# A hybrid decoder layer: attention scores in two fp32r passes, residual spilled, out-projection by tile

## Chip, cores and metric

The kernel runs on one core of a Trainium2 chip. The metric is the device time of one execution in microseconds (us). A TensorE matmul streams up to 512 columns through 128 rows of stored weights; VectorE, ScalarE and GpSimd work on tiles of 128 partitions; DMA queues move tiles between DRAM and SBUF. Every engine carries out its own instructions strictly in the order of its queue and waits for the others through semaphores.

## The reference

One decoder layer of 512 tokens and width 1024 in float32. The mixer in the middle is what the change touches:

```python
x = layer_norm(alpha * x + 0.5 * swiglu_ffn(x, ffn1_w13, ffn1_w2), ln1_g, ln1_b)
gq, gk, gv, gz, ga, gb, dq, dk, dv = jnp.split(x @ w_in, offsets, axis=-1)
y_a = gdn_mixer(gq, gk, gv, gz, ga, gb, ...)         # gated delta rule, 4 heads x 128, gate silu(z)
y_b = diff_attention_mixer(dq, dk, dv, ...)          # 4 heads, two softmax maps of 64 dims each
x = layer_norm(alpha * x + concat(y_a, y_b) @ w_out, ln2_g, ln2_b)
...                                                  # second FFN with a gated embedding, LN3

# diff_attention_mixer, for one block of 128 queries
s = einsum("bqhmd,bkhmd->bhmqk", q, k) * 64 ** -0.5  # m: two maps
s = where(causal, s, -inf); pr = softmax(s, axis=-1)
attn = pr[:, :, 0] - lam * pr[:, :, 1]
o = rms_norm(einsum("bhqk,bkhd->bqhd", attn, v), subln_w) * (1 - lam_init)
```

## The kernel before

The 512 tokens are four tiles of 128 (`NT`). Large products run in three fp32r matmuls (`mm3`, L295 to L299): operands are split into a rounded high part (a ScalarE cast) and the remainder (a VectorE subtract), and hi x hi, hi x lo, lo x hi add up in PSUM. Small products run as fp32 matmuls, each of which the trace shows as two passes.

Three stages follow one another: the first FFN (until about 362 us), the mixers (until about 689 us), the second FFN. At the end of the first, `norm_natural` normalises each token tile in `RES[t]` with VectorE, ScalarE and GpSimd (L302 to L326) and `norm_turn` (L341) transposes it on TensorE.

The mixers (`mix_zone`, L823) begin with the values and gates, then `keys_queries` (L958): for each head a product of 24 matmuls, a convolution on VectorE and a silu on ScalarE into `KQ`, and one unit later `squares`, which turns the unit before (`turn4`, L871) and squares it. What follows is woven from lanes. A lane is a Python generator that yields an estimated cost and a wait; `weave` (L97) takes the first open lane whose time has come, and so fixes the order in which the code is emitted. The framework's scheduler and the rotating buffers (PSUM tags a, b, c of 3, 2 and 3 tiles; 3 raw weight tiles, 4 split ones) then set the order within each engine. The lanes:

- `gdn(c)` (L1057): four chunks of the delta rule; `diagonal` (L1111) inverts 16x16 blocks with 30 VectorE operations (L1129, L1130), going through DRAM before (`ST<-blocks`, L1123) and after (`TT<-blocks`, L1137); `chain` (L1194) carries the state over the chunks (L1202 to L1249) and hands each chunk to `to_mix`, which turns and splits it into `XH`, `XL`.
- `attention(t, h)` (L1144): 16 lanes, one for a query tile and a head. Two scores (L1156, on 64 rows each, keys in `DKT`, queries in `DQT`) and their mask (L1157), the maxima (L1158), exponentials (L1161), difference (L1165), transposes (L1169), the product with `DV` (L1175), a norm with a power on GpSimd (L1182) and the output y (L1183), written over the query.
- `fill` (L995): the projections of keys, queries, values and z, block by block. A key or query tile is rotated on GpSimd, turned on TensorE and copied on VectorE (L1003).
- `out_attn` (L1276) after all heads: four turns, then the attention half of the output product; `out_gdn` (L1285) after it: the other half, LN2.

`TT` (32 rows of blocks, cleared by GpSimd at L851) and `DQT` have tiles of their own. Weights come over SP's DMA queue in order; DMAs of the diagonal go over SP and ScalarE's queue.

## Time and profile before

| | us |
|---|---|
| time, median of three runs (lowest, highest) | 1088.29 (1087.98, 1088.46) |
| the profiled execution | 1089.54 |
| its span on the core | 1087.8 |
| mean granted TensorE clock | 0.998 |

The page gives for each engine the time in which it had an instruction under way. Matmuls overlap in TensorE's pipeline, so a matmul's price is read from the distance between two starts, not from its duration. PE is TensorE, PEld its weight loads, DVE VectorE, ACT ScalarE, POOL GpSimd, SP the queue of most DMAs; an x2 behind an fp32 matmul is its two passes. Idle time stands in brackets or behind "idle", with the instruction that ended it.

### The profile page before, as it was taken

Reading aid. Unit: us, or ns where it says so; the run is one execution under the profiler, and the core shown is the slowest. Engines: PE = TensorE matmul, PEld = TensorE weight load, DVE = VectorE, ACT = ScalarE, POOL = GpSimd, SP = SyncE. Lnnn points to the kernel's source line nnn. Section 1 sums busy time; section 2 is a strip of 40 time slices with the busy share of each in tenths; the row PEclk is TensorE's granted clock in tenths of the full one; section 3 lists DMA queues with packets and bytes.
Section 4 is the critical chain, followed back from the end, with each engine's and each line's share of the span. In section 5 each row is a group of like instructions: output and inputs, shape, how many; then the busy total and the mean of one; then the engine's idle time right before and its main releaser. Section 6 shows DMA issues by size and latency. Waiting matters only on the chain. (4 is left out here: it accounts for less than half of the span.)

```text
span 1087.8 us, 17345 instructions
## 1 busy us (share of the span) xinstructions
PE 1066.9 (98%) x6627; PEld 941.0 (87%) x6627; DVE 827.7 (76%) x1446; ACT 490.8 (45%) x949; POOL 108.6 (10%) x172
## 2 busy tenths in 40 slices
PE   9999999999999999999999999999999999999996
PEld 7889898989897978778865887789899998999895
DVE  5989796979678466357665558899988796979568
ACT  5645353535343266324465632545454453535231
POOL 1100000000002202431112303100000000000003
PEclk9999999999999999999999999999999999999999
DMA  8633232333333042124110211514342433333212
GB/s 290 204 115 118 89 110 94 117 91 109 93 109 106 1 136 87 33 74 108 40 59 1 78 43 54 174 59 146 119 124 79 117 98 90 123 99 98 78 39 97
DMA packets 44275, 106.03 MB, mean 97 GB/s; under 512 B 10848, under 2 KB 12528, under 8 KB 44192
## 3 DMA queue, kind: packets, MB, share of 16 engines
q1 hardware_dynamic: 37968, 96.71, 29.1%
q0 software_dynamic: 1808, 6.04, 1.7%
q10 hardware_dynamic: 4416, 2.16, 0.7%
q8 instruction: 52, 0.85, 0.3%
q14 instruction: 31, 0.25, 0.1%
HBM read 102.41 MB, written 2.49 MB: 96 GB/s over the span
## 5 line engine op out<-in xcount | busy, mean ns | idle before, releaser
L160 DVE TENSOR_TENSOR wl<-raw,wh 128x1024 fp32r<-128x1024 f32 (+3 forms) x137 | 142.8, 1049 | 38.7 <-ACT wh L159 37.5
L159 ACT CAST wh<-raw 128x1024 fp32r<-128x1024 f32 (+3 forms) x137 | 123.0, 905 | 100.3 <-PE pa L298 31.0
L297 PE MATMUL pb<-wh,hh 128*128 128x512 f32 (+1 forms) x356 | 138.5, 390 | 3.7 <-DVE RES L734 1.1
L298 PE MATMUL pb<-wl,hh 128*128 128x512 f32 (+1 forms) x356 | 138.0, 388 | 0.0
L299 PE MATMUL pb<-wh,hl 128*128 128x512 f32 (+1 forms) x356 | 137.8, 387 | 0.0
L229 ACT CAST th<-tr 128x512 fp32r<-128x512 f32 x160 | 98.5, 619 | 85.1 <-PE pc L298 49.8
L233 DVE TENSOR_TENSOR tl<-tr,th 128x512 fp32r<-128x512 f32 x160 | 109.4, 686 | 11.2 <-ACT th L229 10.3
L190 ACT CAST wh<-raw 128x512 fp32r<-128x512 f32 x88 | 54.4, 622 | 134.2 <-PE pb L299 88.1
L297 PE MATMUL pb<-wh,XH 128*128 128x512 f32 (+1 forms) x256 | 101.5, 397 | 1.8 <-ACT wh L159 1.0
L297 PE MATMUL pa<-XH,wh 128*128 128x256 f32 (+1 forms) x344 | 100.0, 291 | 0.1
L298 PE MATMUL pa<-XL,wh 128*128 128x256 f32 (+1 forms) x344 | 100.0, 291 | 0.0
L299 PE MATMUL pa<-XH,wl 128*128 128x256 f32 (+1 forms) x344 | 99.9, 290 | 0.0
L298 PE MATMUL pb<-wl,XH 128*128 128x512 f32 (+1 forms) x256 | 97.6, 381 | 1.2 <-DVE wl L160 1.1
L299 PE MATMUL pb<-wh,XL 128*128 128x512 f32 (+1 forms) x256 | 96.9, 379 | 0.0
L297 PE MATMUL pc<-XH,th 128*128 128x256 f32 x320 | 90.6, 283 | 0.0
L298 PE MATMUL pc<-XL,th 128*128 128x256 f32 x320 | 90.6, 283 | 0.0
L299 PE MATMUL pc<-XH,tl 128*128 128x256 f32 x320 | 90.6, 283 | 0.0
L490 DVE TENSOR_TENSOR RES<-RES,pb 128x512 f32<-128x512 f32 (+1 forms) x81 | 54.6, 677 | 45.2 <-PE pb L299 44.4
L191 DVE TENSOR_TENSOR wl<-raw,wh 128x512 fp32r<-128x512 f32 x88 | 60.2, 690 | 31.7 <-ACT wh L190 31.6
L297 PEld LDWEIGHTS pb<-wh,hh 128*128 128x128 f32 x356 | 66.9, 188 | 19.4 <-DVE RES L734 1.9
L299 PEld LDWEIGHTS pb<-wh,hl 128*128 128x128 f32 x356 | 66.9, 188 | 13.9
L298 PEld LDWEIGHTS pb<-wl,hh 128*128 128x128 f32 x356 | 66.9, 188 | 13.1 <-DVE wl L191 0.3
(312 smaller groups left out, 2665.0 us busy)
## 6 DMA issues: line engine op xcount, KB each, us to landing
raw<-in_wa_dram SPq DMA_DIRECT2D x127, 512.0 KB, 3.7
raw<-in_wb_dram SPq DMA_DIRECT2D x88, 256.0 KB, 2.7
raw<-in_wd_dram SPq DMA_DIRECT2D x4, 520.0 KB, 3.6
RES<-in_xn_dram POOLq DMA_DIRECT2D x4, 512.0 KB, 5.9
gb<-in_gb_dram POOLq DMA_DIRECT2D x8, 256.0 KB, 4.0
xr<-in_xT_dram ACTq DMA_DIRECT2D x7, 256.0 KB, 4.6
out_dram<-RES SPq DMA_DIRECT2D x5, 256.0 KB, 2.1
TT<-in_gb_dram POOLq DMA_DIRECT2D x4, 256.0 KB, 3.6
```

The lines of the kernel that those rows point to most:

```text
L159: return (self.nc.scalar.copy(hi, src), self.nc.vector.tensor_tensor(lo, src, hi.bitcast(F32), ALU.subtract))
L160: self.nc.vector.tensor_tensor(lo, src, hi.bitcast(F32), ALU.subtract))
L190: nc.scalar.copy(hi, r)
L191: nc.vector.tensor_tensor(lo, r, hi.bitcast(F32), ALU.subtract)
L229: act.copy(h, t)
L233: dve.tensor_tensor(hl[1], t, hl[0].bitcast(F32), ALU.subtract)
L297: pe.matmul(o, wh, xh, start=first, stop=False)
L298: pe.matmul(o, wh, xl, start=False, stop=False)
L299: pe.matmul(o, wl, xh, start=False, stop=last)
L490: dve.tensor_tensor(rj, rj, pd, ALU.add)
```

## The change

Scores. `KK` holds for each of the two maps m the high part of the turned keys in this map's 64 rows and the remainder in the other map's rows. `QZ` holds, for four heads in turn, the queries in four slots: slot m has the high part of map m in its own rows and the full query, rounded, in the other rows; slot 2+m has the remainder in its own rows and zeros in the others. A score is then two fp32r matmuls on 128 rows with the same `KK`. `QZ` is written for two heads at once by the even head: two ScalarE casts, two GpSimd casts, two VectorE subtracts. A turned key tile is written by two ScalarE casts and two VectorE subtracts instead of one VectorE copy.

Memory. The residual becomes one tile `RESA`. `TT` lies over its tiles 0 and 1, the queries `DQT` over tiles 2 and 3. So the four residual tiles are stored to DRAM (`XR`) during the third key unit, and loaded again in `out_attn`: 0 and 1 at its start, 2 and 3 after tiles 1 and 3 have been turned. `TT` is cleared after the stores, and the LN2 gains are loaded into `DV` instead of `TT`.

Order. Squares come two units after their unit instead of one; key blocks use PSUM "c"; z is copied and its silu done for two tiles at once; `out_attn` opens when the delta rule's chunks and z are done and takes each tile when its four heads are done; its turns use PSUM "b" and `project_out` yields after every second weight tile; the costs given to `weave` for attention change.

```diff
-        self.RES = [cp.tile([P, D], F32, name=f"RES{t}") for t in range(NT)]
+        self.RESA = cp.tile([P, NT, D], F32, name="RESA")
+        self.RES = [self.RESA[:, t] for t in range(NT)]
...
+        KK = mp.tile([P, 2, H, S], F32R, name="KK")
+        QZ = mp.tile([P, 4, 4, P], F32R, name="QZ")
+        DQT = [self.RESA[:, 2 + t // 2, (t % 2) * 512:(t % 2) * 512 + 512].rearrange("p (h b) -> p h b", b=P)
+               for t in range(NT)]
+        TT = self.RESA[:, 0:2].rearrange("p c (d h b) -> p (c d) h b", d=2, b=P)
...
-        pool.memset(TT, 0.0)
+        XR = dp.tile([NT, P, D], F32, name="XR")
...
-                    if held:
-                        squares(*held)
+                    if len(held) == 2:
+                        squares(*held.pop(0))
...
+                    held.append((i, h))
+                    if i == 0 and h == 2:
+                        for t in range(NT):
+                            nc.sync.dma_start(XR[t], RES[t])
+                    if i == 1 and h == 0:
+                        pool.memset(TT, 0.0)
...
-                    dve.tensor_copy((DKT if word == "k" else DQT)[:, :, t * P:(t + 1) * P], v4(pt))
+                    if word == "k":
+                        for m in range(2):
+                            r, o = rows(m), rows(1 - m)
+                            hi = KK[r, m, :, t * P:(t + 1) * P]
+                            act.copy(hi, v4(pt)[r])
+                            dve.tensor_tensor(KK[o, m, :, t * P:(t + 1) * P], v4(pt)[r], hi.bitcast(F32), ALU.subtract)
+                    else:
+                        dve.tensor_copy(DQT[t], v4(pt))
...
-                    pq = ps("b")
+                    pq = ps("c" if word == "k" else "b")
...
+                act.copy(ZG[:, t], v4(pq))
+                if t % 2:
+                    z = ZG[:, t - 1:t + 1].rearrange("p t h b -> p (t h) b")
+                    act.activation(z, z, AF.Silu)
...
+            i = (t * H + h) % 4
+            qz = QZ[:, i]
+            if h % 2 == 0:
+                two, src = QZ[:, i:i + 2], DQT[t][:, h:h + 2]
+                for m in range(2):
+                    r, o = rows(m), rows(1 - m)
+                    act.copy(two[r, :, m], src[r])
+                    pool.tensor_copy(two[o, :, m], src[r])
+                    dve.tensor_tensor(two[r, :, 2 + m], src[r], two[r, :, m].bitcast(F32), ALU.subtract)
+                said.add(("qz", t, h + 1))
+                yield 0, 2.0
...
-                r = slice(m * DQK, (m + 1) * DQK)
-                pe.matmul(sc[m], DQT[r, h, t * P:(t + 1) * P], DKT[r, h, 0:n], start=True, stop=False)
+                for q in (m, 2 + m):
+                    pe.matmul(sc[m], qz[:, q], KK[:, m, h, 0:n], start=q == m, stop=False)
...
         def out_attn():
-            for t in range(NT):
-                to_mix(DQT[:, :, t * P:(t + 1) * P], t, 4, "c")
-                yield 0.5, 0
+            for t in (0, 1):
+                nc.sync.dma_start(RES[t], XR[t])
             w = [self.take() for _ in range(4)]
             for t in range(NT):
+                while not done[t] <= said:
+                    yield 0, 0.5
+                to_mix(DQT[t], t, 4, "b")
+                if t % 2:
+                    nc.sync.dma_start(RES[2 + t // 2], XR[2 + t // 2])
+                yield 0.5, 1.0
                 yield from project_out(w, 0, t)
...
-        need_out = {("attn",) + th for th in heads} | {"z"}
+        need_out = {("gdn", c) for c in range(NC)} | {"z"}
```

Three places in the order of the instructions. The first is VectorE at the start of attention: the copy of query tile 0 (`DQT`, in `RESA` after), the maxima (`amx`) and the diagonal operations on `ST`. Before:

```order
L1003 COPY DKT<-pb_5080 128x4x128
L1003 COPY DQT<-pb_5119 128x4x128
L1158 TENSOR_REDUCE amx_5132<-pc_5131 128x1
L1129 TENSOR_TENSOR ST_4062<-ST_4061 128x15
L1158 TENSOR_REDUCE amx_5149<-pc_5148 128x1
L1130 TENSOR_TENSOR ST_4061<-ST_4061,ST_4062 128x15
L1129 TENSOR_TENSOR ST_4062<-ST_4061 128x28
L1158 TENSOR_REDUCE amx_5132<-pc_5131 128x1
L1130 TENSOR_TENSOR ST_4061<-ST_4061,ST_4062 128x14x2
```

In the changed kernel, at the place where the copy stands now:

```order
L1153 TENSOR_TENSOR ST_4058<-ST_4057 128x64
L1154 TENSOR_TENSOR ST_4057<-ST_4057,ST_4058 128x8x8
L1153 TENSOR_TENSOR ST_4058<-ST_4057 128x63
L1154 TENSOR_TENSOR ST_4057<-ST_4057,ST_4058 128x7x9
L1022 COPY RESA<-pb_5134 128x512
L1153 TENSOR_TENSOR ST_4058<-ST_4057 128x60
L1154 TENSOR_TENSOR ST_4057<-ST_4057,ST_4058 128x6x10
L1153 TENSOR_TENSOR ST_4058<-ST_4057 128x55
L1180 TENSOR_TENSOR QZ<-RESA,QZ 64x2x128
L1154 TENSOR_TENSOR ST_4057<-ST_4057,ST_4058 128x5x11
L1180 TENSOR_TENSOR QZ<-RESA,QZ 64x2x128
```

The copy L1003, now L1022, stood ahead of the first diagonal operation and now stands behind the eighteenth of them (L1153, L1154); the subtracts into `QZ` (L1180) follow it.

The second is GpSimd at the end of the first FFN, the norms of tiles 2 and 3 (`bnrs`, `RES`) and the clearing of `TT`. Before:

```order
L326 TENSOR_TENSOR RES_70<-RES_70,gb_3795 128x256
L314 TENSOR_TENSOR bnrs_3979<-bnrs_3979,mhalf 128x1
L316 TENSOR_SCALAR bnrs_3979<-bnmv_3977,bnrs_3979 128x1
L325 TENSOR_TENSOR RES_71<-RES_71,gb_3794 128x256
L326 TENSOR_TENSOR RES_71<-RES_71,gb_3795 128x256
L314 TENSOR_TENSOR bnrs_4037<-bnrs_4037,mhalf 128x1
L851 MEMSET TT 128x2048
```

In the changed kernel (`RESA` in L986 is `TT`):

```order
L327 TENSOR_TENSOR RESA<-RESA,gb_3792 128x256
L986 MEMSET RESA 128x2048
L315 TENSOR_TENSOR bnrs_3976<-bnrs_3976,mhalf 128x1
L317 TENSOR_SCALAR bnrs_3976<-bnmv_3974,bnrs_3976 128x1
L326 TENSOR_TENSOR RESA<-RESA,gb_3791 128x256
L327 TENSOR_TENSOR RESA<-RESA,gb_3792 128x256
L315 TENSOR_TENSOR bnrs_4034<-bnrs_4034,mhalf 128x1
```

The memset has moved from behind the last norm to between those of tiles 1 and 2.

The third is TensorE in attention of tile 3. Before, its scores (L1156) stand between the matmuls of the z projection (`pb`):

```order
L297 MATMUL pb_6069<-wh_5427,XH 128x512
L298 MATMUL pb_6069<-wl_5428,XH 128x512
L299 MATMUL pb_6069<-wh_5427,XL 128x512
L297 MATMUL pb_6069<-wh_5729,XH 128x512
L298 MATMUL pb_6069<-wl_5730,XH 128x512
L299 MATMUL pb_6069<-wh_5729,XL 128x512
L1156 MATMUL pc_6048<-DKT,DQT 128x512
L1157 LDWEIGHTS idb
L1157 MATMUL pc_6048<-LVM,idb 128x128
L297 MATMUL pb_6069<-wh_5729,XH 128x512
L1156 MATMUL pc_6049<-DKT,DQT 128x512
L1157 LDWEIGHTS idb
```

In the changed kernel, the scores of the same tile (L1193):

```order
L1239 MATMUL pa_6277<-ST_4058,KQ 128x128 x4
L1247 MATMUL pa_6287<-ST_4058,KQ 128x128 x4
L298 MATMUL pb_6330<-wh_5872,XH 128x512
L299 MATMUL pb_6330<-wl_5873,XH 128x512
L300 MATMUL pb_6330<-wh_5872,XL 128x512
L298 MATMUL pb_6330<-wh_6134,XH 128x512
L299 MATMUL pb_6330<-wl_6135,XH 128x512
L1254 MATMUL pa_6316<-VV,UU 128x128
L300 MATMUL pb_6330<-wh_6134,XL 128x512
L1193 MATMUL pc_6296<-KK,QZ 128x512 x2
L1194 LDWEIGHTS idb
L1194 MATMUL pc_6296<-LVM,idb 128x128
```

Between the scores now stand steps of the chain (L1239, L1247, L1254) and a few matmuls of the output product.

## Rows read from the trace of the kernel before

**Rows 1.** Page, part 1: engine, busy us, share of the span, instructions.
```profile
PE 1066.9 (98%) x6627; PEld 941.0 (87%) x6627; DVE 827.7 (76%) x1446; ACT 490.8 (45%) x949; POOL 108.6 (10%) x172
```

**Rows 2.** Timeline, TensorE: start, duration, line, operation, form, count; scores of tiles 0, 3.
```profile
476.63 0.40 PE L297 MATMUL pb<-wh,XH 128*128 128x512 f32 x1
476.87 0.39 PE L298 MATMUL pb<-wl,XH 128*128 128x512 f32 x1
477.09 0.40 PE L299 MATMUL pb<-wh,XL 128*128 128x512 f32 x1
477.42 0.48 PE L1156 MATMUL pc<-DKT,DQT 64*128 64x128 f32 x2
477.83 0.23 PE L1157 MATMUL pc<-LVM,idb 128*128 128x128 bf16 x1
...
574.75 1.12 PE L1156 MATMUL pc<-DKT,DQT 64*128 64x512 f32 x2
575.81 0.23 PE L1157 MATMUL pc<-LVM,idb 128*128 128x128 bf16 x1
```

**Rows 3.** Timeline, TensorE: the values stage, and eight fp32 passes in gdn.
```profile
359.30 0.28 PE L297 MATMUL pb<-wh,XH 128*128 128x256 f32 x1
359.41 0.28 PE L298 MATMUL pb<-wl,XH 128*128 128x256 f32 x1
...
538.71 1.05 PE L1105 MATMUL pa<-UU,ta 128*128 128x128 f32 x8
539.60 0.60 PE L871 MATMUL pb<-CST,tb 128*128 128x128 f32 x4
```

**Rows 4.** Waits of lines L1156 and L871: TensorE idle until, us, times.
```profile
  DVE DQT L1183: 3.3, 5
...
  ACT KQ L899: 3.9, 7
```

**Rows 5.** Timeline, TensorE, SP, VectorE: diagonal (third row: KB, us to landing).
```profile
468.24 1.46 PE L1071 MATMUL pa<-KQ 128*128 128x256 f32 x6
...
474.10 0.34 SPq L1123 DMA_DIRECT2D ST<-blocks  x1
...
ST<-blocks SPq DMA_DIRECT2D x1, 128.0 KB, 2.8
...
483.65 0.21 DVE L1129 TENSOR_TENSOR ST<-ST 128x63 f32<-128x63 f32 x1
...
484.16 0.22 DVE L1129 TENSOR_TENSOR ST<-ST 128x60 f32<-128x60 f32 x1
```

**Rows 6.** Timeline, GpSimd, TensorE: norms of FFN1 [idle before, releaser].
```profile
355.09 0.98 POOL L314 TENSOR_TENSOR bnrs<-bnrs,mhalf 128x1 f32<-128x1 f32 x1 [1.81 <-DVE bnrs L313]
...
358.53 0.73 POOL L326 TENSOR_TENSOR RES<-RES,gb 128x256 f32<-128x256 f32 x1
...
362.93 1.82 POOL L851 MEMSET TT<- 128x2048 f32 x1 [1.78 <-DVE RES L329]
...
362.13 0.71 PE L341 MATMUL pa<-CST,RES 128*128 128x128 f32 x5
```

**Rows 7.** Windows: busy us by engine, clock, DMA; VectorE's groups: busy, mean, idle.
```profile
573.00:606.00 33.00, 31.94 (x148) 21.02 (x147) 17.43 (x40) 20.37 (x41) 7.73 (x11) 1.00 0.03 3
606.00:657.00 51.00, 49.88 (x295) 41.93 (x295) 30.36 (x67) 21.45 (x67) 8.47 (x9) 1.00 0.25 82
...
L160 DVE TENSOR_TENSOR wl<-raw,wh 128x1024 fp32r<-128x1024 f32 x8 | 9.7, 1253 | 4.5 <-ACT wh L159 4.5
L1272 DVE SCALAR_TENSOR_TENSOR RES<-RES,pb 128x512 f32<-128x512 f32 x8 | 5.5, 684 | 4.9 <-PE pb L299 4.9
```

**Rows 8.** Groups of 430 to 660: count, busy us, mean ns, idle before.
```profile
L1077 POOL TENSOR_TENSOR MP<-MP,CST 128x512 f32<-128x512 f32 x4 | 5.1, 1285 | 14.1 <-DVE MP L1075 14.1
...
L1183 DVE SCALAR_TENSOR_TENSOR DQT<-pc,aso,VEC 128x128 f32<-128x128 f32 x16 | 5.6, 350 | 7.4 <-POOL aso L1182 7.3
```

**Rows 9.** Page, part 6: DMA issues: count, KB each, us to landing.
```profile
raw<-in_wa_dram SPq DMA_DIRECT2D x127, 512.0 KB, 3.7
```

More of the change, by code (lines that the diff above doesn't have):

```diff
@@ L832, in mix_zone @@
         MP = mp.tile([P, 2, NC, H, P], F32, name="MP")
-        TT = mp.tile([P, NC, H, P], F32, name="TT")
         UU = mp.tile([P, NC, H, P], F32, name="UU")
@@ L837, in mix_zone @@
         DV = mp.tile([P, NT, H, P], F32, name="DV")
-        DKT = mp.tile([P, H, S], F32, name="DKT")
-        DQT = mp.tile([P, H, S], F32, name="DQT")
+        KK = mp.tile([P, 2, H, S], F32R, name="KK")
[3 more added lines that the diff above has]
+        TT = self.RESA[:, 0:2].rearrange("p c (d h b) -> p (c d) h b", d=2, b=P)
         ST = [mp.tile([P, H, P], F32, name=f"ST{i}") for i in range(2)]
@@ L967, in squares @@
                     act.copy(KD[:, :, h, :], v4(pt[:, 0:(NC - 1) * P]))
-            held = None
+            held = []
             for i in range(2):
@@ L983, in keys_queries @@
             yield
-            squares(*held)
+            for qh in held:
+                squares(*qh)
             pool.memset(UU, 0.0)
@@ L993, in keys_queries, with rows @@
                 pool.tensor_tensor(NRM[:, c], q1[:, c], phalf[:, 0:H], ALU.pow)
+        def rows(m):
+            return slice(m * DQK, (m + 1) * DQK)
         def fill():
@@ L1011, in fill @@
                             turn(*held)
+                    if word == "q" and t == 0:
+                        for m in range(2):
+                            pool.memset(QZ[rows(1 - m), :, 2 + m].bitcast(F32), 0.0)
                     d = tb()
@@ L1145, in attention @@
             n = (t + 1) * P
+            i = (t * H + h) % 4
+            qz = QZ[:, i]
+            if h % 2 == 0:
+                two, src = QZ[:, i:i + 2], DQT[t][:, h:h + 2]
+                for m in range(2):
+                    r, o = rows(m), rows(1 - m)
[4 more added lines that the diff above has]
+                yield 0, 2.0
             if t < 2:
@@ L1175, in attention @@
                 pe.matmul(po[:, 0:P], at[:, c * P:(c + 1) * P], DV[:, c, h, :], start=c == 0, stop=c == t)
-            y = DQT[:, h, t * P:(t + 1) * P]
+            y = DQT[t][:, h]
             so = stat([P, 4], "aso")
@@ L1268, in project_out @@
                         self.ahead()
-                yield 2.6, 0
+                    if k % 2:
+                        yield 1.3, 0
                 rj = RES[t][:, j * 512:(j + 1) * 512]
@@ L1274, in project_out @@
                     dve.tensor_tensor(rj, rj, pd, ALU.add)
+        done = [{("attn", t, h) for h in range(H)} for t in range(NT)]
         def out_attn():
-            for t in range(NT):
-                to_mix(DQT[:, :, t * P:(t + 1) * P], t, 4, "c")
-                yield 0.5, 0
+            for t in (0, 1):
+                nc.sync.dma_start(RES[t], XR[t])
             w = [self.take() for _ in range(4)]
             for t in range(NT):
+                while not done[t] <= said:
[4 more added lines that the diff above has]
+                yield 0.5, 1.0
                 yield from project_out(w, 0, t)
@@ L1285, in out_gdn @@
         def out_gdn():
-            gbt = [TT[:, j].rearrange("p a b -> p (a b)") for j in range(4)]
+            gbt = [DV[:, j].rearrange("p a b -> p (a b)") for j in range(4)]
             self.load_gb(gbt, G_LN2)
@@ L1316, in attn_ready @@
                 need.add(("attn",) + heads[i - 2])
+            if h % 2:
+                need.add(("qz", t, h))
             return lambda: need <= said
```

7 lines of the change are left out of this document (2 added, 5 removed).

## The prediction

> **What bounds the kernel now.** I read the page's busy shares first. The reader is to see that TensorE is busy for 98% of the span, its weight loads for 87%, and that VectorE, the next, is busy for 76% and ScalarE for 45% [rows 1]. So time is won where TensorE's own instructions get shorter or its few waits go, and lost where a new wait stops it. Then I read TensorE's timeline, which gives the price of a matmul as the distance between two starts (the durations overlap), and the waits of single lines, which tell what TensorE waited for. Last come stretches of the span, for the load of the other engines.
>
> **Scores.** A score matmul L1156 is fp32 on 64 rows and runs as two passes. From its start to the start of the mask matmul L1157 it takes 0.41 us for 128 keys and 1.06 us for 512 [rows 2]. On a straight line 256 and 384 keys take 0.63 and 0.84 us (estimates). There are eight of each size (four heads, two maps), so 8 x 2.94 = 23.5 us. After it, each score is two fp32r matmuls on 128 rows. An fp32r matmul of 512 columns takes 0.23 us [rows 2] and one of 256 columns 0.12 us [rows 3]. No row has one of 384 or of 128: 384 lies between, 0.175; 128 lies between half of 0.12 and half of the fp32 price, 0.06 to 0.205, and I take 0.10, near the half that the fp32r rows suggest. That is 8 x 2 x (0.10 + 0.12 + 0.175 + 0.23) = 10.0 us: **13.5 saved**, 11.8 to 14.1. All of it lies on TensorE, hence on the path while TensorE has other work queued.
>
> Ahead of a score that follows an fp32r matmul there is 0.33 us between starts where 0.23 is usual [rows 2]. This 0.10 should go, since the score becomes what its neighbours are. 32 scores x 0.10: **3 saved**, 0 to 3.2.
>
> **Waits that go.** Before the turns L871, TensorE waits 3.9 us in seven pieces for ScalarE's KQ [rows 4]: the turn for the squares of a key unit comes one unit (24 matmuls of 512 columns, over 5 us) after it. With a held list of two it comes two units after. **3 saved**, 0 to 3.9. Before the scores it waits 3.3 us in five pieces for VectorE's L1183, that is for a "c" tile of PSUM that an earlier head still holds [rows 4]. Shorter scores leave that wait in part and the preparation for two heads at once lets a head come earlier: **2 saved**, 0 to 3.3. Together 13.5 + 3 + 3 + 2 = **21.5**.
>
> **New wait 1: the first QZ.** The order of VectorE puts the copy of query tile 0 behind 18 of the 30 diagonal operations; before, it stood ahead of the first. Those wait for ST<-blocks. Counted from the end of the last preparing matmul L1071 (468.24 + 1.46 = 469.7), this transfer is issued 4.4 us later and lands 2.8 us after that [rows 5]: 7.2. Two diagonal operations take 0.51 us from start to start [rows 5], 18 take 4.6. Then the copy of 512 columns, 0.6 (an estimate: the sum L1272 of 512 columns takes 0.68 [rows 7], less some overlap), then a GpSimd cast of 64x256. Its price is not in the trace: the two-input operation of 128x512 takes 1.28 us [rows 8], so half, 0.64, is above it and a quarter, 0.32, below; I take 0.6, nearer to the row. The score can start at 7.2 + 4.6 + 0.6 + 0.6 = 13.0. TensorE has until then, by the order, 31 fp32r matmuls of 512 columns and two turns of four transposes: 31 x 0.23 + 8 x 0.11 = 8.0. **5 lost**, 0 to 6: the queue of TensorE is in order, so the fill matmuls behind this score can't cover it. Queued behind it are the second half of the query projection and the four gdn lanes. The Trainium skill, in "GPSIMD Engine Reference", section "4.1 Engine selection", holds one-input work on GpSimd to be about at line rate and two-input work about twice as slow, so by it the cast is a half of the two-input row per column, 0.32 us, and the wait 0.3 less; no run here has shown it.
>
> **New wait 2: the residual in RESA.** TT now lies over residual tiles 0 and 1, so its memset (1.82 us) must wait until these are stored, and the order puts it between the norms of tiles 1 and 2 on GpSimd. Before, GpSimd was done with tile 1 at 355.09 - 1.81 = 353.3, did tile 2 from 355.09 to 358.53 + 0.73 = 359.3, TensorE turned tile 2 at 362.13, and the memset stood at 362.93, behind all norms [rows 6]. The store of tile 1 leaves SP when GpSimd is done with it and takes about as long as a load of 512 KB, 3.7 us [rows 9]: the memset runs from 357.0 to 358.8 and tile 2's 4.2 us end at 363.0. **1 lost**, 0 to 4. The stores and the later reloads themselves cost nothing: three weight tiles are in SBUF before the stores, so those behind them on SP are not needed at once, and where the reloads run, DMA is a quarter busy [rows 7].
>
> **New wait 3: attention of tile 3 under the chain.** Before, tile 3's heads and the chain over the chunks followed one another, each with weight matmuls between. Now they are interleaved, and with them stand only 26 matmuls of 512 columns. Counted from the order with the prices above, TensorE has 33 us there: eight scores 4, 42 transposes at 0.11 = 4, 87 fp32 matmuls of 128x128 at 0.22 = 19 (two passes of 0.11: eight passes from 538.71 to 539.60, [rows 3]), and 26 x 0.23 = 6. VectorE was busy for 17.43 us in 573 to 606 and for 30.36 in 606 to 657, ScalarE for 20.37 and 21.45 [rows 7]. Without the weight work of these stretches (VectorE: L160 9.7 us and six output sums L1272 of 0.68 [rows 7], and the first norm), with 2 us of new QZ work, VectorE keeps some 34 us, as much as TensorE, and ScalarE some 27. Two full queues that wait for one another in order lose something at each hand-over. By a hand sequence with distances between starts TensorE stalls 2.6 us, with full durations 7.5, and for the last y of the chain 1.4 to 2.8 more. **5 lost**, 2.6 to 10.3; I take a value nearer to the distances, because the timeline shows that queued operations overlap.
>
> **New wait 4: tiles 0 to 2.** Each pair adds two ScalarE casts, two GpSimd casts and two VectorE subtracts ahead of its scores, and the key fill now also takes "c" tiles. A wait for a "c" tile has lasted 0.66 us (3.3 in 5 pieces, [rows 4]). One for half of the 12 heads is **4 lost**, 2 to 8. **Tail:** by tile, out-projection leaves less work between the last chain step and the norms, and residual 3 comes back (3.7 us for 512 KB [rows 9]) only after to_mix of tile 3: **1.5 lost**, 0 to 4. The silu in pairs, the gains in DV instead of TT and the squares on another unit move ScalarE and GpSimd work that is not on the path: 0, and up to 1 us of either sign.
>
> **Sum.** -21.5 + 5 + 1 + 5 + 4 + 1.5 = -5.0. The profiled execution took 1089.54 us, 1.25 more than the median of 1088.29. So 1084.5 for it, and 1083.3 on the scale of the median.
>
> **Rivals.**
> A: the new waits are hidden. Then TensorE stays the bound throughout: -21.5 and 4 for what is left of them, **1071**. For it: a 98% busy TensorE with short waits [rows 1, 4]. Against: at the first QZ and in tile 3 the order leaves it nothing to do meanwhile. Chance 0.20.
> B, slower: VectorE's queue decides over all of attention and chain. Then the tile 3 stage loses 10.3 instead of 5, the earlier heads 8 instead of 4 and the tail 4 instead of 1.5: 11.8 on top, **1095**. It ends slower than before by more than can be measured once the new waits exceed 23.7 us (21.5 and 0.2% of 1088). For it: VectorE's 34 us beside TensorE's 33 us. Against: in the same two stretches before, it was busy for 48 us of 84 and the waits were tenths. Chance 0.19.
> C: GpSimd becomes the late link. Every head's y waits for a power on GpSimd (L1183 idles 7.3 us for it over 16 heads [rows 8]), and now two casts of a pair can stand ahead: 16 heads x 0.32 = 5 more, **1088**. The Trainium skill, in "GPSIMD Engine Reference", section "1. Specifications", says that GpSimd shares SBUF interfaces with VectorE and contends with its two-input operations; by it VectorE's subtracts would stretch as well, and this chance rises. Chance 0.15.
> That the passes of 128 columns are no cheaper than fp32 is inside the bounds above (1.7 us).
>
> **How the numbers follow.** Forecast 0.46, A 0.20, B 0.19, C 0.15; the likeliest is **1083.3**. Its own range, with its bounds not all at one end, is 1077 to 1088. The range for 8 in 10 takes in most of A and of B: 1072 to 1094. What can be told from no change is 0.2%, 2.2 us: faster is below 1086.1, slower above 1090.5. The forecast gives 0.38 of its 0.46 to faster, A all, C 0.05: 0.63; slower has B and a little of the forecast and C: 0.20; the same 0.17.
>
> **What would show it.** Scores: score to mask at 0.2, 0.24, 0.35 and 0.46 us; if it is above 0.4 for 128 keys, the passes are not cheaper. Wait 1: TensorE idle for about 5 us before the first score, released by ScalarE or GpSimd's QZ, and VectorE's copy behind diagonal operations. Wait 2: an idle of about 1 us before the turn of tile 2. Wait 3: TensorE's busy share falling in the chain, VectorE over 85% there. KQ: no idle before L874 in the key units. If TensorE is busy for 98% again, A holds; if VectorE's rows fill the chain, B. It is wrong if a store, a reload or a weight load lands late, since I price those at nothing.

## The result: 0.6% slower, by TensorE's stops

| | us |
|---|---|
| before, median of four runs (lowest, highest) | 1088.38 (1087.98, 1088.8) |
| after, median of four runs (lowest, highest) | 1095.35 (1093.33, 1096.53) |
| ratio after to before, 95% interval | 1.0058 (1.0045, 1.0070) |
| span of the profiled execution, before and after | 1087.8, 1091.6 |

The forecast was 1083.3 with 1072 to 1094: wrong in sign, and just outside the range. The page of after, part 1, beside [rows 1]:

```profile
PE 1060.1 (97%) x6627; PEld 944.2 (87%) x6627; DVE 836.5 (77%) x1466; ACT 502.2 (46%) x974; POOL 115.9 (11%) x188
```

TensorE is busy for 6.8 us less in a span that is 3.8 us longer. So its work did get shorter, and more than that came in as idle time. The windows show where. First before, then after, both from the end of the values stage to the last norms; the columns are the stretch, its length, busy us of PE, PEld, DVE, ACT and POOL (with instructions), TensorE's granted clock (1.00 is 2.4 GHz), DMA share and GB/s.

```profile
372.00:440.00 68.00, 66.61 (x344) 55.02 (x342) 38.61 (x62) 40.55 (x111) 10.19 (x11) 1.00 0.31 93
440.00:470.00 30.00, 30.00 (x137) 23.85 (x136) 12.84 (x22) 8.15 (x11) 14.28 (x25) 1.00 0.24 71
470.00:515.00 45.00, 44.65 (x250) 35.47 (x249) 30.55 (x100) 15.93 (x48) 12.27 (x30) 1.00 0.31 77
515.00:560.00 45.00, 44.83 (x285) 36.24 (x283) 29.38 (x66) 22.89 (x50) 5.44 (x13) 1.00 0.16 48
560.00:600.00 40.00, 38.94 (x176) 24.89 (x175) 22.34 (x57) 24.33 (x51) 6.79 (x13) 1.00 0.04 14
600.00:650.00 50.00, 49.84 (x308) 43.35 (x307) 30.01 (x62) 24.13 (x65) 9.90 (x10) 1.00 0.17 51
650.00:690.00 40.00, 37.90 (x176) 29.45 (x176) 32.74 (x60) 15.04 (x27) 14.13 (x17) 1.00 0.32 103
```

```profile
372.00:440.00 68.00, 67.59 (x348) 56.51 (x347) 36.98 (x62) 40.82 (x112) 13.35 (x15) 1.00 0.31 94
440.00:470.00 30.00, 29.27 (x133) 23.14 (x131) 16.95 (x27) 11.73 (x17) 14.01 (x21) 1.00 0.26 72
470.00:515.00 45.00, 40.60 (x214) 32.69 (x215) 30.82 (x90) 18.82 (x47) 13.28 (x35) 0.96 0.29 75
515.00:560.00 45.00, 43.05 (x303) 38.54 (x301) 31.65 (x69) 24.57 (x50) 4.50 (x11) 1.00 0.19 59
560.00:600.00 40.00, 35.50 (x195) 28.52 (x195) 23.81 (x57) 27.77 (x64) 11.21 (x17) 0.96 0.18 54
600.00:650.00 50.00, 46.05 (x281) 37.21 (x280) 30.42 (x86) 22.77 (x75) 10.28 (x18) 1.00 0.13 43
650.00:690.00 40.00, 38.30 (x171) 29.04 (x170) 34.00 (x55) 12.60 (x17) 11.34 (x14) 1.00 0.31 101
```

Length less busy PE, summed over the seven stretches, is 5.2 us before and 17.6 after. The key units (first row) idle 1.0 us less. Everything lost lies between 440 and 650: 1.7 us of idle time before, 15.5 after. The clock column says that in two stretches TensorE also ran below 2.4 GHz for a part of the time: 45 x 0.04 = 1.8 us and 40 x 0.04 = 1.6 us are lost to it. Before, no stretch shows that.

**The scores are as short as forecast.** Timeline of after, TensorE, from a score to its mask matmul, for 128, 256 and 512 keys, beside [rows 2]:

```profile
483.39 0.39 PE L300 MATMUL pb<-wh,XL 128*128 128x512 f32 x1
483.61 0.33 PE L1193 MATMUL pc<-KK,QZ 128*128 128x128 f32 x2
483.79 0.23 PE L1194 MATMUL pc<-LVM,idb 128*128 128x128 bf16 x1
...
531.59 0.48 PE L1193 MATMUL pc<-KK,QZ 128*128 128x256 f32 x2
531.91 0.23 PE L1194 MATMUL pc<-LVM,idb 128*128 128x128 bf16 x1
...
604.24 0.71 PE L1193 MATMUL pc<-KK,QZ 128*128 128x512 f32 x2
604.79 0.23 PE L1194 MATMUL pc<-LVM,idb 128*128 128x128 bf16 x1
```

From score to mask it takes 0.18, 0.32 and 0.55 us, where 0.20, 0.24 and 0.46 were forecast (other scores of these sizes: 0.25, 0.24 and 0.57) and 0.41 and 1.06 stood before for 128 and 512. The distance from the fp32r matmul ahead to the score is 0.22 instead of 0.33: the gap is gone too. The longer of these figures stand behind an fp32 matmul, which a score now follows after 0.03 us and followed after 0.20 in before. So 512 keys, from the start of that matmul to the mask, take 0.58 us (604.21 to 604.79) where before took 1.26 (574.55 to 575.81): 0.68 less, forecast 0.70 with the gap.

**Two stops, and what stands behind each.** The first, in TensorE's timeline and ScalarE's (start, duration, line, operation, form, count, idle before and releaser):

```profile
468.87 0.40 PE L300 MATMUL pb<-wh,XL 128*128 128x512 f32 x1
471.57 0.50 PE L298 MATMUL pb<-wh,XH 128*128 128x512 f32 x1 [2.30 <-ACT tb L1035]
```

```profile
468.38 1.90 ACTq L1139 DMA_DIRECT2D blocks<-MP  x4
470.33 0.58 ACT L1019 CAST KK<-pb 64x512 fp32r<-64x512 f32 x1 [1.84 <-issue]
470.93 0.59 ACT L1035 COPY tb<-pb 128x512 f32<-128x512 f32 x1
```

TensorE wants a "b" tile of PSUM. The copy that frees it (L1035) stands on ScalarE's queue behind a cast of the new key parts and behind four DMA issues of the diagonal, which hold that queue for 1.90 us. This cast is new; the four issues stood there in the kernel before too. The second stop:

```profile
589.56 0.83 PE L1212 MATMUL pc<-DV,tt 128*128 128x128 f32 x6
593.64 1.16 PE L1264 MATMUL pa<-ta,KD 128*128 128x128 f32 x8 [3.25 <-ACT ta L1256]
```

```profile
589.70 1.05 ACT L160 CAST wh<-raw 128x1024 fp32r<-128x1024 f32 x1
590.76 1.28 ACT L1066 ACT_TABLE_LOAD   x1
592.06 1.06 ACT L1066 ACTIVATE MP<-MP 128x1024 f32<-128x1024 f32 x1
593.02 0.57 ACT L1256 COPY ta<-pa 128x512 f32<-128x512 f32 x1
```

The chain's copy of X is again ScalarE's, behind weight casts for the out-projection and z's silu with its table load. Behind both stops the windows of 4 us show the clock falling:

```profile
472.00:476.00 4.00, 4.00 (x12) 3.14 (x11) 1.74 (x9) 0.00 (x0) 1.27 (x4) 0.57 0.12 33
...
592.00:596.00 4.00, 2.36 (x17) 2.36 (x18) 1.25 (x3) 3.87 (x10) 2.74 (x3) 0.88 0.74 248
596.00:600.00 4.00, 4.00 (x23) 3.22 (x23) 3.21 (x8) 1.62 (x10) 1.85 (x3) 0.69 0.01 2
```

4 x 0.43 = 1.7 us in the first place, 4 x (0.12 + 0.31) = 1.7 in the second: at 1.2 GHz the fp32r matmuls that started after 472.51 stand 0.43 us apart instead of 0.23.

**Heads come late.** The first score of tiles 1, 2 and 3 starts at 501.20, 544.50 and 574.75 in before, and at 531.59, 563.52 and 597.09 in after. With the last tile 22 us late, the projections that should have stood between its scores are over: between its first and last score TensorE has 33 weight matmuls in before, 12 in after.

### The profile page after: what moved, and what is told of

The parts are those of the page before. It is cut to its first block, busy times and chain, and to the rows that moved or that the text cites. A ratio compares the mean times of both kernels' runs of the same rounds, so it can differ in the third digit from the quotient of the medians.

```text
span 1091.6 us, 17453 instructions
## 1 busy us (share of the span) xinstructions
PE 1060.1 (97%) x6627; PEld 944.2 (87%) x6627; DVE 836.5 (77%) x1466; ACT 502.2 (46%) x974; POOL 115.9 (11%) x188
## 4 chain that ended last, share of the span: by engine, by line
PE 55%; DVE 5%; ACT 3%; POOL 2%; DMA 2%; issue 1%; ACTq 0%; DVEq 0%; SPq 0%; POOLq 0%
PE pb L298 7%; PE pb L300 7%; PE pb L299 7%; PE pc L300 6%; PE pc L298 6%; PE pc L299 6%; PE pa L300 3%; PE pa L299 3%; PE pa L298 3%; ACT wh L160 1%; DMA raw<-in_wa_dram 1%; PE pc L1193 1%; PE pa L874 1%; PE pa L1113 1%; DVE wl L161 1%
## 5 line engine op out<-in xcount | busy, mean ns | idle before, releaser
L234 DVE TENSOR_TENSOR tl<-tr,th 128x512 fp32r<-128x512 f32 x160 | 109.7, 687 | 11.2 <-ACT th L230 10.3
L298 PE MATMUL pb<-wh,XH 128*128 128x512 f32 (+1 forms) x224 | 88.1, 393 | 6.4 <-ACT tb L1035 2.3
L491 DVE TENSOR_TENSOR RESA<-RESA,pb 128x512 f32<-128x512 f32 (+1 forms) x81 | 54.6, 677 | 45.2 <-PE pb L300 44.4
L299 PE MATMUL pb<-wl,XH 128*128 128x512 f32 (+1 forms) x224 | 85.9, 383 | 1.5 <-DVE wl L161 1.3
L300 PE MATMUL pb<-wh,XL 128*128 128x512 f32 (+1 forms) x224 | 85.5, 382 | 0.5 <-DVE aso L1217 0.5
```

Source lines behind the costliest of these rows:

```text
L234: dve.tensor_tensor(hl[1], t, hl[0].bitcast(F32), ALU.subtract)
L298: pe.matmul(o, wh, xh, start=first, stop=False)
L299: pe.matmul(o, wh, xl, start=False, stop=False)
L300: pe.matmul(o, wl, xh, start=False, stop=last)
L491: dve.tensor_tensor(rj, rj, pd, ALU.add)
```

## Experiments

Each kernel was timed beside the kernel before on the same chip; the ratio to it is given with its 95% interval, and ratios are what is compared. For after it is 1.0058 (1.0045, 1.0070). The suspects: out-projection by tile; ScalarE's queue at the two stops; the preparation of `QZ` inside the heads; the memory plan; the new scores themselves; the smaller edits.

### Out-projection, the two stops, the scores alone

**e1_out_late** is after with the out-projection as before: when all heads are done, four turns first.

```diff
-            w = [self.take() for _ in range(4)]
             for t in range(NT):
-                while not done[t] <= said:
-                    yield 0, 0.5
-                to_mix(DQT[t], t, 4, "b")
+                to_mix(DQT[t], t, 4, "c")
...
+            w = [self.take() for _ in range(4)]
+            for t in range(NT):
                 yield from project_out(w, 0, t)
...
-        need_out = {("gdn", c) for c in range(NC)} | {"z"}
+        need_out = {("attn",) + th for th in heads} | {"z"}
```

> The changed kernel with the out-projection woven as before: it opens after all sixteen heads, turns the four tiles first, and yields once per half. Everything else of the change stays. Theory S (ScalarE's queue stops TensorE at two places, and the granted clock falls to 1.2 GHz behind each stop): the X copy no longer stands behind four weight casts and tile 3's stage gets its weight matmuls back, so the 3.25 us stop at 590 and the slow clock behind it go, and about half of the small waits after 597: 1095 less 6 to 9, 1086 to 1089. Rival V (VectorE's queue decides over attention and chain, whatever stands beside it): VectorE has the same work, 1093 to 1096. Rival D (the first stop, before attention, is most of the loss): 1092 to 1094.

Measured: 1.0088 (1.0070, 1.0106), slower still. No weight matmul is left between the scores of tile 3, and 600 to 650 has a clock of 0.93. So in after the out-projection by tile is what little fill tile 3 has; undoing it alone does not help.

**e2_sp_only** takes the four DMA issues off ScalarE's queue.

```diff
-                (nc.scalar if b % 2 else nc.sync).dma_start(
+                nc.sync.dma_start(
```

> The changed kernel with the eight stores of the diagonal blocks all on SP's queue, none on ScalarE's. Theory S: the 2.30 us stop at 469 goes, since the copy that frees the PSUM tile no longer stands behind four DMA issues (1.9 us), and with it the half clock from 472.1 to 475.5 (about 1.7 us): 1095 less 2 to 4, 1091 to 1093. Rival Q (the first QZ decides, as the prediction had it): TensorE gets to the first score some 4 us earlier and waits there for it instead, in idle time before L1193; the time stays within 1 us of 1095, and it is longer by the later diagonal transfer if that counts.

Measured: 1.0059 (1.0042, 1.0076), no gain that can be told; the intervals leave room for 2 us either way. Waits of TensorE in 330 to 700 (waiting line, releaser: us in all, times, longest), first after, then e2:

```profile
PE pb L298 <- ACT tb L1035: 2.3, 1, 2.3
...
PE pc L1193 <- DVE amx L1195: 1.7, 3, 0.7
```

```profile
PE pc L1193 <- DVE amx L1195: 3.0, 2, 2.2
...
PE pb L298 <- ACT tb L1035: 1.2, 1, 1.2
```

The stop is halved, so the issues make half of it, and the matmuls behind it stay 0.23 us apart. The first score starts at 476.45 instead of 479.66. Then 2.2 us go to one wait for VectorE's maxima. The block of the delta rule that starts at 512.63 in after starts at 510.03, so this trace keeps 2.6 us. It is, however, the fastest of e2's four runs (1090.15, median 1093.33), and the ratio shows nothing of it.

**e4_x_dve** takes the copy of X of chunk 0 to VectorE.

```diff
-                act.copy(X, px)
+                (act.copy if c else dve.tensor_copy)(X, px)
```

> The changed kernel with one instruction moved: the copy of X of chunk 0 out of PSUM is done by VectorE instead of ScalarE. In VectorE's order it stands ahead of the last weight remainder, so it can run at about 590.2 instead of 593.0. Theory S: the stop of 3.25 us before L1264 shrinks to under 0.7, the clock stays at 2.4 GHz from 592 to 599 (1.7 us): 1095 less 3 to 4.5, 1090.5 to 1092. Rival V: VectorE is the bound there, a copy more on it costs 0.6 and the wait moves to the next reader: 1094 to 1096.

Measured: 1.0051 (1.0034, 1.0068), no gain that can be told. The wait ahead of L1264 falls from 3.25 to 0.45 us, but the first scores of tile 3 then wait 1.70 us for VectorE's y, and the clock, still 1.00 in 592 to 596, is 0.57 in 596 to 600.

**e8_scores** has the new scores and the memory plan only: out-projection, squares, z and the key blocks' PSUM tag as before; after's costs for the planner are kept.

```diff
-                    if len(held) == 2:
+                    if len(held) == 1:
...
-                    pq = ps("c" if word == "k" else "b")
+                    pq = ps("b")
...
+                z = tb()
+                act.activation(z, pq, AF.Silu)
```

> The scores and the memory plan alone: KK, QZ, residual spilled and reloaded; the out-projection, the silu of z, the squares and the PSUM tag of the key blocks as before the change. Theory S: the stop at 469 stays with its clock (4 us), the one at 590 goes; scores 13 us shorter, QZ and small waits 6 to 8 more: 1088 less 1 to 5, 1083 to 1087. Rival V: attention's own hand-overs eat what the passes save, 1089 to 1094.

Measured: 1.0124 (1.0109, 1.0139), the slowest of all. The new scores with their preparation inside the heads (and after's planner costs) cost 13 us here, where I had forecast a gain of 13.5 for them.

### Preparation in its own lanes

**e9_prep_lane** is after with the six instructions on `QZ` in lanes of their own. Such a lane opens when the pair two before is done, and a head only waits for it.

```diff
+        def prepare(t, h):
...
+            yield 0, 2.0
+            said.add(("qz", t, h))
+            said.add(("qz", t, h + 1))
+
         def attention(t, h):
...
-            if h % 2 == 0:
-                two, src = QZ[:, i:i + 2], DQT[t][:, h:h + 2]
...
+        lanes += [Lane(prepare(*heads[i]), prep_qz_ready(i)) for i in range(0, 16, 2)]
```

> The changed kernel with the preparation of QZ taken out of the attention lanes into lanes of its own: a pair is prepared as soon as the pair before the last is done, while the last one is still under way, instead of at the head of its own lane. Same instructions, another order. Theory L (latency: the preparation stands in the dependent chain of every pair, eight times, so the sixteen heads finish after the projections that should run beside them are used up, and tile 3 stands bare): by the order, 53 weight matmuls stand between tile 3's scores instead of 12, so the stops from 580 to 660 and the slow clock there go: 1095 less 8 to 15, 1080 to 1087. Theory S (two places in ScalarE's queue): the stop at 469 stays, the one at 590 may go with the order: 1090 to 1092. Rival V (VectorE decides): 1093 to 1097.

Measured: 1.0038 (1.0024, 1.0052), 2.2 us below after, though the intervals overlap at their ends. The first score of tile 3 (597.09 in after) in e9's timeline of TensorE:

```profile
574.67 0.71 PE L1196 MATMUL pc<-KK,QZ 128*128 128x512 f32 x2
```

That is where it stood in before (574.75, [rows 2]), and 53 weight matmuls stand between tile 3's scores instead of 12. This settles why the heads were late: inside the head, the preparation adds its wait to every pair, and the planner, which takes the first lane that is open, fills it with the delta rule's pieces, ahead of the scores in TensorE's queue. In after TensorE does nothing but these (L1113 to L1129, with their turns) from 512.63 to 531.44, and tile 1's first score comes behind them. The block itself isn't new: much the same pieces stand from 511 to 531 in before and in e9, but there four and two of tile 1's eight scores come ahead of it or near its start.

**e10_fp32** is the opposite: after with the old fp32 scores, all else kept.

```diff
-                for q in (m, 2 + m):
-                    pe.matmul(sc[m], qz[:, q], KK[:, m, h, 0:n], start=q == m, stop=False)
+                r = rows(m)
+                pe.matmul(sc[m], DQT[t][r, h], DKT[r, h, 0:n], start=True, stop=False)
```

> The changed kernel without the new scores: scores as fp32 on 64 rows with DKT, no KK, no QZ, the planner's cost of attention as before; residual spilled, out-projection by tile, silu in pairs, squares two units late and key blocks in PSUM c stay. Theory L: 13.5 us more of TensorE work than the changed kernel, but no preparation and the order of the heads as before the change: nearly no stops, full clock, 1084 to 1088, faster than the changed kernel by 7 or more though its passes are longer. Rival W (out-projection by tile and the spill cost the time): 1094 or more. Theory S: the stop at 469 goes too, since it needs the key casts on ScalarE: 1088 to 1092.

Measured: 1.0063 (1.0045, 1.0081), clock 0.998. So with the old scores (and the old planner costs for attention) the rest of the change is as slow as after. What it waits for (same columns):

```profile
PE pb L298 <- ACT XH L160: 2.4, 3, 1.1
...
PE pb L300 <- DVE XL L161: 1.1, 1, 1.1
```

That is the out-projection by tile: a turn on TensorE, ScalarE's cast, VectorE's remainder, and at once the product that needs them.

**e11_prep_sp_xd** joins e9, e2 and e4.

> The three edits together: QZ in lanes of its own, all stores of the diagonal blocks on SP, X of chunk 0 copied by VectorE. Theory L with S: both gains add, since they are at different places: 1076 to 1083, faster than before the change. Theory L alone: as the kernel with the preparation lanes, within 1 us. Rival V: 1092 to 1096.

Measured: 1.0023 (1.0011, 1.0035), median 1089.57 us where 1076 to 1083 was forecast for both gains: 0.15% below e9, and the intervals overlap.

### Out-projection again, with the heads in time

**e13_prep_late** is e9 with e1's edit, **e14_prep_late_sp** e13 with e2's.

> QZ prepared in lanes of its own, and the out-projection woven as before the change (after all heads, four turns first). Theory T (two separate losses: the preparation inside each pair's chain, and, in out-projection by tile, the chain of turn, ScalarE cast, VectorE remainder and product, for which TensorE waits at every tile): 1091.3 with the lanes alone, less 4 to 7, 1084 to 1087. Rival N (undoing the out-projection gives nothing, as with the preparation left in the heads, where it went from 1095.4 to 1096.6): 1091 to 1093.

> The same with all stores of the diagonal blocks on SP's queue. Theory T with the stop at 469 (2.3 us and the half clock behind it) as a third loss: 1.5 to 3 below the kernel without it, 1081 to 1085, and faster than the kernel before the change. Rival Q (the first QZ is waited for instead): as the kernel without it, within 1 us.

Measured: 1.0001 (0.9992, 1.0011) and 0.9986 (0.9976, 0.9995). With the heads in time, the late out-projection gains 0.37% (4.0 us) over e9, and now the stop that e2 shortens is worth something, 1.6 us (the intervals overlap a little). Against e1, which has the same out-projection, the preparation's lanes gain 0.87%: 9.5 us.

**e15_prep_pipe_sp** keeps the out-projection by tile, but turns each tile ahead of the product of the tile before (with the lanes and SP's stores; e11 without the edit of X).

```diff
+                for u in ((0, 1) if t == 0 else (t + 1,)):
+                    if u < NT:
...
+                        to_mix(DQT[u], u, 4, "b")
```

> QZ in lanes of its own, stores on SP, and out-projection by tile, but the turn of the next tile is written ahead of the product of the current one. Theory T: the waits for the cast and the remainder of XH and XL (2.4 and 1.1 us with fp32 scores) go since a product lies between: 1083 to 1087. Rival U (by tile is slow because attention, chain and out-projection compete, not because of the turn): 1088 to 1091.

Measured: 0.9992 (0.9983, 1.0002), about e14. Against e11's 1.0023, the order by tile loses because product follows turn at once, not because it is by tile: 0.31%, 3.4 us.

**e16_fp32_late** is e10 with the late out-projection.

> Fp32 scores and the out-projection as before the change; residual spilled and reloaded, silu in pairs, squares two units late, key blocks in PSUM c stay. Theory T: these parts cost nothing and the squares give 1 to 2 us: 1085 to 1088. Rival M (the memory plan costs, by its stores, the memset or the reloads): 1090 to 1094, and then the out-projection by tile costs less than thought.

Measured: 1.0027 (1.0016, 1.0038), 0.36% below e10: the same gain as from e9 to e13. Against e13 it says that in that form the new scores, with their lanes, bring 0.26%, 2.8 us, of the 13.5.

### The clock, the memory plan, the small edits

**e17_keep_busy** is after with twelve added fp32r matmuls of 512 columns (2.8 us on TensorE) in the second stop; their result is overwritten.

```diff
+                    if c == 0:
+                        with self.behind([last]):
+                            for _ in range(12):
+                                pe.matmul(pk, KK[:, 0, 0, 0:P], KK[:, 0, 1, :], start=True, stop=True)
```

> The changed kernel with twelve fp32r matmuls of 512 columns more, 2.7 us, whose result is overwritten: TensorE runs them where it stands still for 3.25 us before L1264 of chunk 0. The output is the same. Theory K (the clock falls because TensorE stood still, and the slow stretch behind it costs about 1.7 us): granted clock 1.00 from 592 to 600, X still arrives when it did, and the time falls by 1 to 2 us although 2.7 us of work were added: ratio to before 1.004 to 1.005 instead of 1.0058. Rival (the clock is a mark of something else, or falls anyway): same clock, time the same or up to 1 us longer.

Measured: 1.0060 (1.0040, 1.0080), unchanged. Timeline and a window of e17:

```profile
589.85 2.78 PE L1266 MATMUL pa<-KK 128*128 128x512 f32 x11
593.14 1.16 PE L1268 MATMUL pa<-ta,KD 128*128 128x128 f32 x8 [0.51 <-ACT ta L1256]
...
596.85 1.11 PE L1239 MATMUL pa<-ST,KQ 128*128 128x128 f32 x8
...
601.15 0.49 PE L1254 MATMUL pa<-VV,UU 128*128 128x128 f32 x2 [1.14 <-DVE VV L1241]
```

```profile
632.00:636.00 4.00, 3.47 (x9) 2.60 (x9) 2.07 (x7) 0.58 (x1) 1.73 (x4) 0.57 0.61 204
```

The same window in after:

```profile
632.00:636.00 4.00, 3.12 (x13) 2.31 (x14) 3.02 (x10) 0.59 (x1) 2.68 (x6) 1.00 0.78 245
```

The clock stays at 1.00 through 592 to 600, and TensorE reaches L1239 2.1 us earlier (598.93 in after). Then it waits 1.14 us for VectorE's VV, for which after did not stop there, and at 632 the clock falls where after kept it. So about half of the lead went to VectorE's chain and the rest to a fall that had only moved. e17 has as many falls as after, so what one fall less is worth isn't shown.

**e18_spill** is before with the memory plan alone: residual to DRAM and back, `TT` and `DQT` over it.

> The kernel before with the memory plan alone: residual in one tile, stored to DRAM and reloaded, TT and the queries over it, LN2's gains in DV; scores fp32, out-projection, silu of z, squares and PSUM tags as before. Theory P (the small parts cost the 3 us that fp32 scores with the old out-projection take over the kernel before): within 1 us of before, 1086.5 to 1088. Rival M (the spill costs them): 1089.5 to 1091.

Measured: 1.0000 (0.9990, 1.0010). Stores, reloads and the memset behind them cost nothing that can be told from 1 us.

**e19_z1** is e14 with z's silu by single tiles, **e21_z1_kb_sq1** e19 with the squares one unit late and the key blocks on PSUM "b", as before.

> QZ in lanes of its own, stores on SP, out-projection as before the change, and the silu of z for one tile at a time instead of two. Theory P with the silu as the costly part (a pair is 1.06 us plus a table load of 1.28 in one piece in front of the copies that heads and chain wait for): 1085.5 less 1.5 to 3, 1082.5 to 1084. Otherwise: 1085 to 1087.

> The same with the squares one unit late and the key blocks in PSUM b as well, as in the kernel before. If the key blocks in c or the squares cost time: 1 us or more below the kernel with the silu undone alone. If the squares two units late give the 1.4 us by which the key stage got shorter: 1 to 2 us above it.

Measured: 0.9985 (0.9974, 0.9996), so the pairs of z do nothing; and 1.0001 (0.9990, 1.0011), so squares and "c" tiles bring some 1.7 us between them, at the edge of what the intervals tell apart. e21 holds the memory plan, the new scores, the lanes and SP's stores, and is level with e18, which has fp32 scores: between these two the shorter scores bring nothing that can be told.

### What holds the last heads

**e22_q_act** is e14 with the copy of query tile 0 on ScalarE, away from the diagonal operations; **e23_q_act_b** also gives the transposes and products of tile 3's last two heads PSUM "b".

```diff
-            pt = ps("c")
+            pt = ps("b" if t == 3 and h > 1 else "c")
...
-            po = ps("c")
+            po = ps("b" if t == 3 and h > 1 else "c")
```

> QZ in lanes of its own, stores on SP, out-projection as before the change, and the copy of query tile 0 done by ScalarE, which stands idle there, instead of VectorE behind the diagonal operations. If the first QZ is still what TensorE waits for (3.5 us of waits from 480 to 500, slow clock at 490): 1085.5 less 1 to 3, 1082.5 to 1084.5. If it waits for the rest of the heads' first steps, the subtracts and maxima, which VectorE does between the diagonal operations as before: 1085 to 1086.

> The same, and the transposes and products of the last two heads of tile 3 use PSUM tag b instead of c. If the waits before those transposes (1.9 and 1.4 us) come from the tag alone: 1 to 3 below the kernel without it. If the heads' own chain is what is late: within 1 us of it.

Measured: 0.9990 (0.9980, 0.9999), nothing; and **0.9968 (0.9954, 0.9982)**, median 1083.48 us: faster than both kernels. Waits of TensorE, e22 and then e23:

```profile
PE pc L1209 <- DVE RESA L1223: 3.3, 2, 1.9
```

```profile
PE pc L1209 <- DVE RESA L1223: 1.4, 1, 1.4
```

L1209 is the transpose of a head's probabilities; it waited for "c" tiles that earlier heads held until their y. From after to e23 it is 0.90%, 9.8 us: in this order 2.2 from the lanes, 4.0 from the late out-projection, 1.6 from SP's stores, 2.0 from the last two edits. The second and the third showed no gain when they were made alone (e1, e2).

## Why the prediction was wrong

What failed is the step from TensorE's work to the span. Two terms of the sum were mis-sized, the waits that go (5 booked, 1.0 found) and wait 3 (5 booked, 8.8 found), and two losses had no term: the lower clock (3.4 us, inside the figures below) and the matmul time that each added stop costs beside its idle time (about 2.4).

**Scores, -13.5, and gap, -3: right as TensorE work**, as shown above. But "on the path while TensorE has other work queued" held in too few places: between kernels that differ in the scores and their preparation, e16 and e13, 2.8 us of it reached the time; between e18 and e21 (which also has SP's stores), nothing that can be told.

**KQ, -3, and score waits, -2: mis-sized from the start.** The views of [rows 4] add the idle time of two queues, matmuls and weight loads. On the matmul queue alone, before waited for KQ once, and for the "c" tile twice (waits of before, 372 to 690):

```profile
PE pc L1156 <- DVE DQT L1183: 1.1, 2, 0.5
...
PE pa L871 <- ACT KQ L899: 1.0, 1, 1.0
```

All idle time of matmuls between 372 and 690 was 5.2 us, in 12 stops, so 5 us from two of its causes were not to be had; these two had 2.1. The key units gained 1.0. The scores' waits didn't go: after has 1.7 us for maxima alone.

**Wait 1, +5: its chain was right, its place was not.** `ST` landed by 473.98, 6.6 us after the last L1095 where 7.2 were forecast; the 18 diagonal operations took 4.4 (4.6), the copy 0.69 (0.6), a GpSimd cast 0.39 to 0.49 (0.6). But TensorE came late itself, after the stop at 468.87 and the slow stretch, which no step held; of the waits for QZ, the first scores' rows keep 0.24 us. So TensorE lost 4 us there (2.3 in the stop, 1.7 to the clock), near the 5 forecast, but to another cause. **Wait 4, +4**, for tiles 0 to 2, can't be parted from it. Together: 9 forecast; idle time in 440 to 560 rose by 6.6, and 1.8 came from the clock: 8.4. That the sum came out near is luck: ScalarE's queue and the clock were not in it.

**Wait 3, +5: mis-sized, with another cause.** 560 to 650 idles 8.45 us where before had 1.2, and loses 1.6 to the clock: 8.8, within my bounds of 2.6 to 10.3, at their upper part. The hand sequence saw that only 26 weight matmuls stand there, but took each hand-over as a small stop of TensorE against VectorE. The largest stop, 3.25 of the 8.45 us, was a copy behind 3.4 us of ScalarE's other work, a wait that the prediction did not have. But e4 brought that stop down to 0.45 us and was no faster that can be told. What e9 shows behind it are the late heads, through latency carried from pair to pair.

**Wait 2, +1: nothing.** The memset held GpSimd from 356.42 to 358.2, near the forecast (357.0 to 358.8), but TensorE shows no idle time ahead of the turn of tile 2, and e18 is level. (This turn stands at 361.48, 0.65 earlier than in before [rows 6], but that lead was there by 85 us: in before TensorE waits 1.15 us at 67.75, in after it does not.) **Tail, +1.5:** 650 to 690 idles 0.4 less than before.

With these sizes: -13.5 - 3 - 1.0 + 8.4 + 8.8 - 0.4 = -0.7. The span rose by 3.8, but the mixers by more: from a matmul that both kernels have near their start (361.53 and 360.88) to one behind them (708.96 and 713.95) after takes 5.6 us longer, for the same number of matmuls. The difference is won outside the change, 0.65 in the first FFN and most of the rest at one wait in the second, which after doesn't have. Before:

```profile
781.71 0.50 PE L297 MATMUL pb<-wh,hh 128*128 128x512 f32 x1 [1.00 <-DVE RES L807]
```

Of the 6.3 between -0.7 and 5.6, about 2.4 are in the stops themselves: the rows count idle time from an operation's end, but an fp32r matmul of 0.40 us normally has its successor after 0.23, so each of 14 more stops (26 against 12) costs 0.17 more than its row says. For the rest, a count from start to start helps, with the median distance of each pair of forms as its price (an estimate from these two traces): the matmuls themselves -14.9 (16.5 was forecast), 28 stops of over 0.15 us against 14 (on this longer stretch) +15.4, the slow clock +3.0, shorter stops and the rest +2.1, together 5.6. And the traced pair is a close one: before's traced execution, 1089.54, lies above its four timed runs, after's is the fastest of its four, so the medians lie 7.0 apart.

**Rivals.** B gave the right time, 1095, by luck (it put 4 on the tail, which lost nothing), and half of the reason: VectorE's maxima, y and VV are where part of the gain of e2, e4 and e17 ended. But VectorE was not full: 30.42 of 50 us in 600 to 650, not over 85%. The runs point to latency in a chain of four engines, not to one engine's load; no run parts the two. A fell with the idle time. C fell too: the y operations wait 6.0 us for GpSimd's power, in before 7.3 [rows 8].

What stays open: why e16 is 0.27% above e18, when both have fp32 scores and a late out-projection and differ in the small edits only (z's silu, the squares, the key blocks' tag), which in e19 and e21 cost nothing. The planner's costs for attention and the split of the keys were never varied alone. How much of the 13.5 us can be had at best is open too: e23 ends 3.5 us below before.

## What to carry to other kernels

Before a saving on the busiest engine is booked, read the idle time of that engine's own matmul queue (not of its weight loads), and ask what latency the edit adds per iteration of a dependent chain: six short instructions off the critical engine delayed the last tile by 22 us, and with it went the filler work that hides the chain. Put such preparation where it can run an iteration ahead (2.2 us here alone, 9.5 with the late out-projection), and let a product follow its operands' turn by at least one other piece of work (3.4 us). A stop that is filled or removed alone may show no more than where the next wait is; judge it again when the chain behind it is short.

## What the hardware showed that I had not expected

- TensorE's clock fell to 1.2 GHz after stops of 2.30 and 3.25 us in an execution that was otherwise dense, and each fall took 1.7 us of TensorE's time. In before, the longest stop between 372 and 690 was 1.0 us, and none of the seven stretches is below 1.00. But the longest stop doesn't decide alone. e9 has the same stop of 2.30 us and keeps 1.00 behind it (its timeline and window):

```profile
470.58 0.50 PE L298 MATMUL pb<-wh,XH 128*128 128x512 f32 x1 [2.30 <-ACT tb L1035]
```

```profile
472.00:476.00 4.00, 4.00 (x22) 3.32 (x21) 2.66 (x14) 0.00 (x0) 0.38 (x1) 1.00 0.09 32
```

  And e14 is at 0.57 in 496 to 500 after three short stops, of 0.41, 0.80 and 0.58 us at 492.75, 494.51 and 495.60.
- Four DMA issues on ScalarE's queue held it for 1.90 us, and with it the PSUM copy behind them.
- VectorE's operations on 128x60 and 128x55 took twice as long beside GpSimd's casts (timelines of VectorE and GpSimd in after):

```profile
478.99 0.21 DVE L1153 TENSOR_TENSOR ST<-ST 128x60 f32<-128x60 f32 x1
479.23 0.45 DVE L1154 TENSOR_TENSOR ST<-ST,ST 128x60 f32<-128x60 f32 x1
479.72 0.42 DVE L1153 TENSOR_TENSOR ST<-ST 128x55 f32<-128x55 f32 x1
```

```profile
479.21 1.95 POOL L1179 CAST QZ<-RESA 64x256 fp32r<-64x256 f32 x4 [5.86 <-DVE ST L1153]
```

  The Trainium skill, in "GPSIMD Engine Reference", section "1. Specifications", has the two engines share SBUF interfaces and contend where VectorE reads two inputs from SBUF; by it the trace agrees, 0.45 and 0.42 us against 0.21 to 0.22 for the same operations without a cast beside them.
